# A parallel attention and linear-attention block: row maximum on other engines, sums one step later, linear outputs kept in two parts

## The chip, the cores and the metric

The kernel runs on one core of one Trainium2 chip. The metric is device time in microseconds (us): the median of several executions. A profiled execution is timed too, and the trace that is read here comes from it. The engines are named as in the profile: PE is TensorE's matmuls, PEld its weight loads, DVE is VectorE, ACT is ScalarE, POOL is GpSimd, and SP is the engine whose queue issues most transfers.

## The reference

One decoder block on 1024 tokens of width 1024, in float32. All projections come from one product with the input weights.

```python
h = rmsnorm(x, g_in)
c_q, c_kv, k_r, z_mla, q_g, k_g, v_g, a_lr, z_gla, gate_mla, gate_gla = split(h @ w_in)
# softmax attention on latent vectors, 8 heads, 64 + 32 rotary columns, causal
q = rope(rmsnorm(c_q) @ w_uq);  k, v = rmsnorm(c_kv) @ w_ukv (k with rope(k_r))
o_mla = softmax(mask(q k^T / sqrt(96))) v
y_mla = (o_mla * silu(z_mla)) @ w_proj_mla
# gated linear attention, 4 heads of 128 by 256, in chunks
log_a = log_sigmoid(a_lr @ w_gla_gate + b) / 16
o_gla = rmsnorm(linear_attention(q_g, k_g, v_g, log_a))
y_gla = (o_gla * silu(z_gla)) @ w_proj_gla
x = x + (sigmoid(gate_mla) * y_mla + sigmoid(gate_gla) * y_gla) @ w_out
return rmsnorm(x, g_final)
```

## The kernel before

The 1024 tokens are worked in two halves `h` of 512 (`TH`), one after the other. To keep float32 accuracy every operand of a large product is split into a rounded part (`hi`) and the remainder (`lo`), and `mm3` (L201) multiplies hi by hi, hi by lo and lo by hi. `split` (L210, L211) makes the parts: a cast on ScalarE and a subtract on VectorE, or on GpSimd if it is asked for.

All projections are units of one list (`Stream`): a unit loads its weights on SP's queue (L170) into one of two raw buffers, splits them (the cast at L187, the subtract at L188), and runs groups of mostly six matmuls. `st.step` gives the next group, and the other stages call it between their own steps, so that TensorE has projection matmuls to do while the attention's small steps run on other engines. `st.upto` runs all units up to a named one. The order of the instructions of each engine is laid down at build time: the framework is asked for a schedule by a simulated timeline (`schedule_with_timeline_sim=True`), with program order as the priority. On the chip every engine then runs its list in that order.

Each half has four stages.

- Start: the latent projections, the rotary tables and the decay (`decay`), which multiplies by the split gate weights `wgs` (L693) and scans with the reset row `rst` (L703). In the first half `consts` and `consts2` load the constants first, each through a staging tile of its own (`graw`, `onraw`, `sraw`).
- Linear attention, four heads (`core`). At its end each of eight feature blocks is scaled and gated into `uo` (L832) and stored in DRAM as `ugd` on SP's queue (L834).
- Softmax attention, eight heads. `row_max` makes a first, rough score product (L886) per block of 128 queries, adds the causal mask on the diagonal (L891) and takes the row maximum (L893). In the second half there are two parts of the row, whose maxima are joined (L897). The negative maximum is split into two rounded columns `mt` (L901, L902), turned by four small matmuls (L907) and copied by ScalarE into two extra rows of the query operand (L910), against which the key operand holds ones. So the score product (L930) has the maximum subtracted. `scores` then takes the exponential (L939), splits it (L942, L943) and adds it up on GpSimd (L945). The product with the values (L951, L952) is put on the list `late`, to be issued a step later; after a head's last product `finish` reads the result (L961, L962), splits the summed weights `ah` (L210, L211), and puts the product of those sums with ones (L968, L969) on the list, two steps later. `tick` counts the steps; a step is one tile of 128 keys, four to a head in the first half and eight in the second. It takes entries from the front of the list only:

```python
while late and late[0][0] <= tick_no[0]:
    late.pop(0)[1]()
```

- From the sixth head on `linear_inputs` brings the linear outputs back: one of two buffers `zr`, shared with the gate units, is loaded from `ugd` (L991) and split (L993, the subtract on GpSimd) into the latent tiles that are no longer used. After that come the output projections (L546 to L548) and the final norm.

SP's queue carries the weight loads, the stores to `ugd` and the loads from it; each waits there for its buffer. ScalarE's queue issues the gate stores, GpSimd's the key and value spills.

Of the kernel before, what the change touches and what calls it, by code (L numbers as in the profile page):

```python
# [7 lines left out]
F32 = mybir.dt.float32  # L8
F32R = mybir.dt.float32r
# [7 lines left out]
P = 128  # L17
# [110 lines left out]
def hybrid_mla_gla_block_kernel(ctx: ExitStack, tc: tile.TileContext, x, xt, pos, vec, gfin, wf, wv, wgate,  # L128
# [87 lines left out]

    def vcol(base, i=0):
        return vecs[:, base + i:base + i + 1]
# [3 lines left out]
    wgs = mk(cst, [P, 512], F32R, "wgs")  # L222
    rst = mk(cst, [P, TH], F32, "rst")
    msk = mk(cst, [P, 3, P], F32, "msk")
    onh = mk(cst, [P, 256], F32R, "onh")
# [15 lines left out]
    ugd = dram.tile([8, P, TH], F32, tag="ugd", name="ugd")  # L241
# [60 lines left out]
    def units_of(h):  # L302
# [16 lines left out]
        def latent_unit(tag, i, u0):  # L319
            @unit(f"{tag}{i}", wunit(u0 + i), "gpsimd")  # L320
            def _(w):
                yield from proj(c, w)
                if i == 0:
                    c.craw[tag] = (mk(c.pp, [P, 3, TH], F32, "craw" + tag), mk(c.pp, [P, 3, TH], F32, "csq"))
# [268 lines left out]
    def consts(bp):  # L593
# [4 lines left out]
        nc.vector.tensor_tensor(out=wgs[64:96, :], in0=graw[64:96], in1=R(wgs[64:96, :]), op=ALU.subtract)  # L598
        nc.vector.tensor_scalar(out=ggh, in0=vecs[:, V_GGLA:V_GGLA + 2], scalar1=0.5, scalar2=None, op0=ALU.mult)

    def consts2(bp):
        nc.sync.dma_start(out=rst, in_=rst_d)
        nc.sync.dma_start(out=msk, in_=msk_d)
        nc.vector.tensor_copy(out=idr, in_=idn)
        oraw = mk(bp, [P, 256], F32, "onraw")
        nc.sync.dma_start(out=oraw, in_=onh_d)
        nc.vector.tensor_copy(out=onh, in_=oraw)
        sraw = mk(bp, [48, 4, P], F32, "sraw")
# [3 lines left out]
    for h in range(2):  # L612
# [6 lines left out]
        gps = pool("glaps", 1, PSUM, stack=gs)  # L619
        um = mk(up, [P, 4, TH], F32, "um")  # L620
# [14 lines left out]
        with ExitStack() as ss:  # L635
            if h == 0:
                with ExitStack() as bs:
# [16 lines left out]
                    consts(bp)  # L654
                    for _ in pro:
                        pass
                    consts2(bp)
            c.pp = pp = pool("start", 1, stack=ss)
# [90 lines left out]
        with ExitStack() as gs2:  # L749
# [3 lines left out]
            def core(g):  # L753
# [71 lines left out]
                for vt in range(2):  # L825
# [8 lines left out]
                    nc.sync.dma_start(out=ugd[f], in_=uo)  # L834
# [9 lines left out]
        with ExitStack() as as_:  # L844
# [28 lines left out]
            def row_max(hd):  # L873
# [8 lines left out]
                for t in range(4):  # L882
                    parts = [TH] * h + [(t + 1) * P]
                    for b, n in enumerate(parts):
# [5 lines left out]
                        if b == len(parts) - 1:  # L890
                            nc.vector.tensor_tensor(out=ps[:, n - P:n], in0=ps[:, n - P:n], in1=msk[:, 1, :],  # L891
                                                    op=ALU.add)
                        nc.vector.reduce_max(mx[:, t, b:b + 1], ps[:, 0:n], axis=mybir.AxisListType.X)  # L893
                    yield
                if h == 1:
                    m1 = mk(ap2, [P, 4, 1], F32, "m1")
                    nc.vector.tensor_tensor(out=m1, in0=mx[:, :, 0:1], in1=mx[:, :, 1:2], op=ALU.max)  # L897
                else:
                    m1 = mx[:, :, 0:1]
# [265 lines left out]
```

## Time and profile before

| what | us |
|---|---|
| median of 3 executions | 1083.74 (1082.48 to 1083.81) |
| the profiled execution | 1085.81 |
| its span, first to last instruction | 1084.0 |
| TensorE's matmuls busy | 1048.3 |
| VectorE busy | 714.0 |
| ScalarE busy | 542.1 |
| GpSimd busy | 374.9 |

The span is that of the profiled execution, 1.8 us below its own time, and all rows below are read from it. Matmuls overlap in the engine's pipeline, so a row's mean duration of a matmul is longer than the time from one to the next. An idle time in brackets is that of the engine before the instruction, with the instruction or transfer that ended it.

### The profile page before, as it was taken

How to read it: one execution, taken by the hardware profiler on the slowest of the kernel's cores; microseconds unless marked ns; L12 is line 12 of the kernel's file. 1: busy time of each engine (PE TensorE's matmuls, PEld its weight loads, DVE VectorE, ACT ScalarE, POOL GpSimd, SP SyncE). 2: the span in 40 equal slices, each digit the busy share in tenths (PEclk: the TensorE clock that was granted, in tenths of full speed). 3: DMA queues.
4: the chain of work that ended last, by engine and by line, in shares of the span. 5: the costliest groups of instructions: out<-in, count | busy, mean ns of one | idle time of the engine just before them, and what ended most of it. 6: DMA issues, size and time to landing. Idle time of an engine off the chain costs nothing.

```text
span 1084.0 us, 14078 instructions
## 1 busy us (share of the span) xinstructions
PE 1048.3 (97%) x5231; PEld 872.4 (80%) x5231; DVE 714.0 (66%) x1114; ACT 542.1 (50%) x910; POOL 374.9 (35%) x274
## 2 busy tenths in 40 slices
PE   8999999999999989999999999999999998999997
PEld 5798998987778867888889989988777776788875
DVE  5796555557586776466887655455767877667673
ACT  5744334455556653444574444344664656553232
POOL 2361121114445542230524211104454656533420
PEclk8899999999999999999999999999999999899999
DMA  8213213235433446644412233235422223424532
GB/s 297 98 59 97 97 60 117 97 100 195 139 98 111 144 139 250 226 138 144 165 60 78 78 102 101 80 112 158 122 96 70 81 83 121 125 90 161 175 111 98
DMA packets 46118, 132.05 MB, mean 122 GB/s; under 512 B 5232, under 2 KB 7664, under 8 KB 45920
## 3 DMA queue, kind: packets, MB, share of 16 engines
q1 hardware_dynamic: 37760, 113.96, 32.1%
q0 software_dynamic: 3680, 8.78, 3.0%
q10 hardware_dynamic: 4608, 8.39, 2.1%
q8 instruction: 41, 0.67, 0.3%
q14 instruction: 29, 0.24, 0.1%
HBM read 110.01 MB, written 21.10 MB: 121 GB/s over the span
## 4 chain that ended last, share of the span: by engine, by line
PE 77%; DVE 12%; ACT 4%; issue 2%; DMA 2%; POOL 1%; SPq 0%; POOLq 0%; DVEq 0%; ACTq 0%
PE pj L201 58%; DVE pl L943 2%; PE y L548 2%; PE y L546 2%; PE y L547 2%; PE ops L201 2%; DVE mx L893 1%; PE sc L930 1%; PE sc L932 1%; PE sc L933 1%; PE ov L951 1%; PE ov L952 1%; PE sc L886 1%; PE at L201 1%; DVE wlo L188 1%
## 5 line engine op out<-in xcount | busy, mean ns | idle before, releaser
L201 PE MATMUL pj<-xl,whi 128*128 128x512 f32 x800 | 301.0, 399 | 1.4 <-DVE xl L282 1.4
L201 PE MATMUL pj<-xh,whi 128*128 128x512 f32 x672 | 270.5, 403 | 2.4 <-ACT whi L187 1.6
L187 ACT CAST whi<-wraw 128x1024 fp32r<-128x1024 f32 (+1 forms) x151 | 155.3, 1029 | 122.0 <-PE pj L201 91.3
L201 PEld LDWEIGHTS pj<-xl,whi 128*128 128x128 f32 x800 | 153.5, 192 | 31.9 <-DVE xl L282 2.9
L201 PE MATMUL pj<-xh,wlo 128*128 128x512 f32 x672 | 176.6, 397 | 0.0
L188 POOL TENSOR_TENSOR wlo<-wraw,whi 128x1024 fp32r<-128x1024 f32 (+2 forms) x52 | 118.2, 2274 | 140.8 <-ACT whi L187 67.4
L201 PEld LDWEIGHTS pj<-xh,whi 128*128 128x128 f32 x672 | 129.7, 193 | 28.0 <-ACT whi L187 1.9
L201 PEld LDWEIGHTS pj<-xh,wlo 128*128 128x128 f32 x672 | 127.2, 191 | 26.3
L188 DVE TENSOR_TENSOR wlo<-wraw,whi 128x1024 fp32r<-128x1024 f32 x100 | 127.4, 1275 | 21.5 <-ACT whi L187 21.3
L945 POOL TENSOR_TENSOR acc<-acc,p 128x512 f32<-128x512 f32 (+3 forms) x80 | 84.9, 1061 | 86.0 <-ACT p L939 70.5
L943 DVE TENSOR_TENSOR pl<-p,ph 128x512 fp32r<-128x512 f32 (+3 forms) x80 | 70.3, 886 | 23.4 <-ACT ph L942 23.2
L939 ACT ACTIVATE p<-sc 128x512 f32<-128x512 f32 (+3 forms) x80 | 37.3, 468 | 68.8 <-DVE sc L935 50.8
L201 PE MATMUL pj<-wlo,xh 128*128 128x256 f32 x256 | 64.4, 285 | 0.0
L201 PE MATMUL pj<-whi,xh 128*128 128x256 f32 x256 | 64.2, 284 | 0.0
L893 DVE TENSOR_REDUCE mx<-sc 128x1 f32<-128x512 f32 (+2 forms) x96 | 51.8, 551 | 11.6 <-PE sc L886 10.4
L548 PE MATMUL y<-whi,zl 128*128 128x512 f32 x128 | 50.5, 396 | 0.5 <-DVE zl L211 0.5
L547 PE MATMUL y<-wlo,zh 128*128 128x512 f32 x128 | 50.4, 395 | 0.0
L546 PE MATMUL y<-whi,zh 128*128 128x512 f32 x128 | 49.5, 396 | 0.0
L201 PEld LDWEIGHTS pj<-wlo,xh 128*128 128x128 f32 x256 | 49.0, 191 | 0.3
L201 PEld LDWEIGHTS pj<-whi,xh 128*128 128x128 f32 x256 | 48.9, 191 | 0.3
L211 POOL TENSOR_TENSOR ql<-qi,qh 128x512 fp32r<-128x512 f32 x8 | 12.4, 1554 | 93.5 <-ACT qh L210 93.5
L349 DVE TENSOR_TENSOR zr<-pj,rbc 128x512 f32<-128x512 f32 x32 | 22.0, 688 | 33.8 <-PE pj L201 33.5
(298 smaller groups left out, 2101.6 us busy)
## 6 DMA issues: line engine op xcount, KB each, us to landing
wraw<-in_dram SPq DMA_DIRECT2D x141, 512.0 KB, 3.5
gtd<-zr ACTq DMA_DIRECT2D x32, 256.0 KB, 2.2
zr<-gtd SPq DMA_DIRECT2D x32, 256.0 KB, 2.9
xr<-in_dram SPq DMA_DIRECT2D x8, 512.0 KB, 9.4
ugd<-uo SPq DMA_DIRECT2D x16, 256.0 KB, 2.2
zr<-ugd SPq DMA_DIRECT2D x16, 256.0 KB, 3.1
xo<-in_dram SPq DMA_DIRECT2D x8, 512.0 KB, 5.8
xs<-in_dram SPq DMA_DIRECT2D x7, 512.0 KB, 8.6
```

The lines of the kernel that those rows point to most:

```text
L187: nc.scalar.copy(out=hi[:, 0:n], in_=raw[:, 0:n])
L188: getattr(nc, lo_engine).tensor_tensor(out=lo[:, 0:n], in0=raw[:, 0:n], in1=R(hi[:, 0:n]), op=ALU.subtract)
L201: nc.tensor.matmul(out=ps, lhsT=a, rhs=b, start=(i == 0), stop=(i == 3 * n - 1))
L211: (lo_engine or nc.vector).tensor_tensor(out=lo, in0=src, in1=R(hi), op=ALU.subtract)
L349: nc.vector.tensor_tensor(out=zr, in0=c.ps, in1=c.rbc, op=ALU.mult)
L546: nc.tensor.matmul(out=c.ops[t], lhsT=a[0], rhs=b[0], start=(k == 0), stop=False)
L547: nc.tensor.matmul(out=c.ops[t], lhsT=a[0], rhs=b[1], start=False, stop=False)
L548: nc.tensor.matmul(out=c.ops[t], lhsT=a[1], rhs=b[0], start=False, stop=(k == 7))
L893: nc.vector.reduce_max(mx[:, t, b:b + 1], ps[:, 0:n], axis=mybir.AxisListType.X)
L939: nc.scalar.activation(p[:, 0:n], ps[:, 0:n], AF.Exp, scale=SCALE)
L943: nc.vector.tensor_tensor(out=pl[:, 0:n], in0=p[:, 0:n], in1=R(ph[:, 0:n]), op=ALU.subtract)
L945: nc.gpsimd.tensor_tensor(out=s.acc[:, q0:TH], in0=s.acc[:, q0:TH], in1=p[:, 0:n], op=ALU.add)
```

## The change

There are four parts and some moves of memory.

- `row_max`: the mask is a row `mrow` of zeros with the diagonal mask in its last 128 columns. One VectorE instruction adds its tail to the scores and takes the maximum; in the second half it starts from the maximum of the row's first part, so that the joining step goes. The two columns `mt` become the same value, minus half the maximum, by one ScalarE instruction of eight columns; the two extra rows add up to the whole.
- `finish`: the sums are due three steps later in the first half and four in the second, in place of two.
- `core`: the linear output is split there, with a cast on ScalarE and a subtract on VectorE, and `ugd` holds both parts (512 KB a block in place of 256 KB). `linear_inputs` loads the two parts straight into their places.
- Memory: `wgs` and `rst` live in the pool of the linear stage. `wgs` is stored once in DRAM and loaded again in the second half, `rst` is loaded in both. The constants share the staging tile `graw`, and the key latents' raw tile has two blocks in place of three.

```diff
+    def move(out, in_, queue=None):
+        (queue or nc.sync).dma_start(out=out.bitcast(F32), in_=in_.bitcast(F32))
-    wgs = mk(cst, [P, 512], F32R, "wgs")
-    rst = mk(cst, [P, TH], F32, "rst")
+    mrow = mk(cst, [P, TH], F32, "mrow")
-    ugd = dram.tile([8, P, TH], F32, tag="ugd", name="ugd")
+    wgd = dram.tile([96, 512], F32R, tag="wgd", name="wgd")
+    ugd = dram.tile([8, P, 2, TH], F32R, tag="ugd", name="ugd")
...
-                    c.craw[tag] = (mk(c.pp, [P, 3, TH], F32, "craw" + tag), mk(c.pp, [P, 3, TH], F32, "csq"))
+                    c.craw[tag] = (mk(c.pp, [P, 2 if tag == "ckv" else 3, TH], F32, "craw" + tag), mk(c.pp, [P, 3, TH], F32, "csq"))
...
+        move(wgd, wgs[0:96])
...
-        nc.sync.dma_start(out=rst, in_=rst_d)
         nc.sync.dma_start(out=msk, in_=msk_d)
+        nc.vector.memset(mrow, 0.0)
+        nc.vector.tensor_copy(out=mrow[:, TH - P:TH], in_=msk[:, 1, :])
         nc.vector.tensor_copy(out=idr, in_=idn)
-        oraw = mk(bp, [P, 256], F32, "onraw")
+        oraw = mk(bp, [P, 512], F32, "graw")[:, 0:256]
...
-        sraw = mk(bp, [48, 4, P], F32, "sraw")
+        sraw = mk(bp, [P, 512], F32, "graw")[0:48].rearrange("p (a b) -> p a b", a=4)
...
+        wgs = mk(gp, [P, 512], F32R, "wgs")
+        rst = mk(gp, [P, TH], F32, "rst")
...
+            if h == 1:
+                move(wgs[0:96], wgd)
+            nc.sync.dma_start(out=rst, in_=rst_d)
...
-                    nc.sync.dma_start(out=ugd[f], in_=uo)
+                    u2 = mk(gb, [P, 2, TH], F32R, "u2")
+                    split(u2[:, 0, :], u2[:, 1, :], uo)
+                    move(ugd[f], u2)
...
-                            nc.vector.tensor_tensor(out=ps[:, n - P:n], in0=ps[:, n - P:n], in1=msk[:, 1, :],
-                                                    op=ALU.add)
-                        nc.vector.reduce_max(mx[:, t, b:b + 1], ps[:, 0:n], axis=mybir.AxisListType.X)
+                            nc.vector.tensor_tensor_reduce(out=ps[:, 0:n], in0=ps[:, 0:n], in1=mrow[:, TH - n:TH], scale=1.0,
+                                                           scalar=NEG if b == 0 else mx[:, t, 0:1], op0=ALU.add,
+                                                           op1=ALU.max, accum_out=mx[:, t, b:b + 1])
+                        else:
+                            nc.vector.reduce_max(mx[:, t, b:b + 1], ps[:, 0:n], axis=mybir.AxisListType.X)
                     yield
-                if h == 1:
-                    m1 = mk(ap2, [P, 4, 1], F32, "m1")
-                    nc.vector.tensor_tensor(out=m1, in0=mx[:, :, 0:1], in1=mx[:, :, 1:2], op=ALU.max)
-                else:
-                    m1 = mx[:, :, 0:1]
                 mt = mk(ap2, [P, 4, 2], F32R, "mt")
-                nc.vector.tensor_scalar(out=mt[:, :, 0:1], in0=m1, scalar1=-1.0, scalar2=None, op0=ALU.mult)
-                nc.vector.scalar_tensor_tensor(out=mt[:, :, 1:2], in0=m1, scalar=-1.0, in1=R(mt[:, :, 0:1]),
-                                               op0=ALU.mult, op1=ALU.subtract)
+                nc.scalar.activation(mt, mx[:, :, h:h + 1].broadcast_to([P, 4, 2]), AF.Copy, scale=-0.5)
...
-                late.append((tick_no[0] + 2, sums))
+                late.append((tick_no[0] + 3 + h, sums))
...
-                    ur = mk(up, [P, TH], F32, "zr", bufs=2)
-                    nc.sync.dma_start(out=ur, in_=ugd[f])
                     hi, lo = slots[2 * f], slots[2 * f + 1]
-                    split(hi, lo, ur, nc.gpsimd)
+                    move(hi, ugd[f][:, 0, :])
+                    move(lo, ugd[f][:, 1, :])
```

## Rows read from the trace of the kernel before

**Rows 1.** The page, busy us, share of span, instructions: TensorE.

```profile
PE 1048.3 (97%) x5231; PEld 872.4 (80%) x5231; DVE 714.0 (66%) x1114; ACT 542.1 (50%) x910; POOL 374.9 (35%) x274
```

**Rows 2.** Stretches: length, busy us of each engine, PEclk, DMA share, GB/s.

```profile
120.00:160.00 40.00, 40.00 (x251) 35.93 (x250) 22.47 (x37) 17.45 (x34) 6.73 (x5) 1.00 0.28 92
...
240.00:434.00 194.00, 186.66 (x865) 150.32 (x864) 134.56 (x235) 108.80 (x179) 90.02 (x70) 0.99 0.46 152
750.00:990.00 240.00, 226.75 (x1014) 180.50 (x1013) 179.02 (x295) 137.20 (x233) 129.06 (x96) 0.98 0.33 99
380.00:410.00 30.00, 27.07 (x123) 21.31 (x122) 22.20 (x42) 17.38 (x33) 14.68 (x14) 0.94 0.39 118
...
905.00:935.00 30.00, 26.04 (x107) 20.33 (x106) 20.19 (x33) 19.20 (x34) 20.83 (x16) 0.89 0.44 132
```

**Rows 3.** Waits of TensorE: releaser, total us, times, longest us.

```profile
PE sc L907 <- DVE mt L902: 4.4, 4, 2.0
...
PE sc L886 <- ACT p L939: 2.0, 1, 2.0
PE rs L969 <- DVE ah L211: 1.8, 4, 0.9
...
PE rs L968 <- ACT ah L210: 1.5, 2, 1.3
PE ov L951 <- DVE um L962: 1.4, 1, 1.4
...
PE sc L930 <- ACT qt L910: 1.4, 4, 0.6
```

**Rows 4.** Timeline around 829 (start us, us): VectorE, GpSimd, TensorE.

```profile
826.65 0.95 DVE L901 TENSOR_SCALAR mt<-m 128x4 fp32r<-128x4 f32 x1
827.64 1.45 DVE L902 SCALAR_TENSOR_TENSOR mt<-m,mt 128x4 fp32r<-128x4 f32 x1
...
827.55 1.52 POOL L188 TENSOR_TENSOR wlo<-wraw,whi 128x640 fp32r<-128x640 f32 x1
...
829.24 0.40 PE L907 MATMUL sc<-idr,mt 128*2 128x128 f32 x4 [1.99 <-DVE mt L902]
```

**Rows 5.** Instructions of tile dec on ScalarE: ns min/median/max.

```profile
L368 ACT ACTIVATE dec<-dex x8: 189/206/214, 66.5 to 651.1; 128x5 f32<-128x5 f32 x8
```

**Rows 6.** Groups by line: count, busy us, mean ns, idle before.

```profile
L187 ACT CAST whi<-wraw 128x1024 fp32r<-128x1024 f32 (+1 forms) x151 | 155.3, 1029 | 122.0 <-PE pj L201 91.3 <-DMA wraw<-in_dram 15.7 <-issue 7.5
...
L893 DVE TENSOR_REDUCE mx<-sc 128x1 f32<-128x512 f32 (+2 forms) x96 | 51.8, 551 | 11.6 <-PE sc L886 10.4
...
L891 DVE TENSOR_TENSOR sc<-sc,msk 128x128 f32<-128x128 f32 x64 | 18.0, 290 | 6.4 <-PE sc L886 6.1
...
L902 DVE SCALAR_TENSOR_TENSOR mt<-m,mt 128x4 fp32r<-128x4 f32 x8 | 8.2, 1026 | 0.3
...
L801 ACT ACTIVATION_READ_ACCUMULATOR junk<-oraw 128x1 f32 x32 | 6.0, 188 | 0.0
...
L901 DVE TENSOR_SCALAR mt<-m 128x4 fp32r<-128x4 f32 x8 | 4.5, 561 | 0.3
```

**Rows 7.** Chain that ended last, 425 to 480: start us, us, what.

```profile
434.16 30.56 PE pj L201 x132
```

**Rows 8.** Timeline around 394: ScalarE, GpSimd, VectorE, TensorE.

```profile
391.23 0.62 ACT L210 CAST qr<-zr 128x512 fp32r<-128x512 f32 x1 [0.89 <-DMA zr<-ugd]
...
391.93 1.29 POOL L211 TENSOR_TENSOR qr<-zr,qr 128x512 fp32r<-128x512 f32 x1 [0.72 <-ACT qr L210]
...
392.41 1.36 DVE L943 TENSOR_TENSOR pl<-acc,ph 128x512 fp32r<-128x512 f32 x1 [1.65 <-ACT ph L942]
...
396.29 0.54 PE L886 MATMUL sc<-kb,qt 96*128 96x512 f32 x1 [1.97 <-ACT p L939]
```

**Rows 9.** Instructions of line L211, VectorE subtract: ns min/median/max.

```profile
L211 DVE TENSOR_TENSOR zl<-zr,zh x16: 692/905/1782, 458.4 to 1045.9; 128x512 fp32r<-128x512 f32 x16
```

**Rows 10.** Waits of SP's queue: releaser, total us, times, longest us.

```profile
SPq L834 <- DVE uo L832: 75.8, 15, 11.4
```

More of the change, by code (lines that the diff above doesn't have):

```diff
@@ L590, in hybrid_mla_gla_block_kernel, with consts @@
         st.fences |= {f"{h}{u}" for u in ("misc", "uqr", "hi0", "hi1", "hi2", "hi3", "yg0", "ym0", "wo00")}
-    def consts(bp):
+    def consts(bp, wgs):
         graw = mk(bp, [P, 512], F32, "graw")
@@ L653, in hybrid_mla_gla_block_kernel @@
                         next(pro)
-                    consts(bp)
+                    consts(bp, wgs)
                     for _ in pro:
```

## The prediction

> **What bounds the kernel now.** I read the page's busy times first. TensorE's matmuls fill nearly the whole span [rows 1], and the change adds or removes none of them: what it can win is only TensorE's idle time and its time at the lower clock. So I then asked for stretches. In the linear-attention stage TensorE never stops while VectorE and ScalarE are about half idle, as in the stretch from 120 [rows 2]; work put there is covered. In the two softmax-attention stages TensorE misses 194.00 - 186.66 = 7.3 us of the first and 240.00 - 226.75 = 13.25 us of the second, 20.6 us in all [rows 2]. VectorE is busy for 134.56 + 179.02 = 314 of those 434 us (72%), the fullest of the other engines.
>
> The last column but two of that view is the granted clock. It is below 1.00 in three places inside attention, each after a cluster of idle gaps: 0.94 over 30 us around 395 (a stretch around 830 reads the same), and 0.89 over 30 us around 920 [rows 2]. That is the lower level, 1.2 GHz, for part of each stretch. Lost there: 0.06 x 30 + 0.06 x 30 + 0.11 x 30 = 6.9 us. The most that any edit here can give back is thus 20.6 + 6.9 = 27.5 us; the start, the tail and the rest of the schedule are not touched by it.
>
> The list of waits says which releaser ends TensorE's gaps [rows 3]; all six lines lie in attention. They are the terms of the sum below.
>
> **The maximum's two roundings become one ScalarE step.** Removed: per head a multiply and a subtract on four columns on VectorE, for the second half also the maximum of two partial maxima. Added: one ScalarE copy with scale, of eight columns. The gap of 1.99 us before the transposes at 829.24 shows what this is worth [rows 4]: the two VectorE instructions begin at 826.65 and end at 829.09, 2.4 us for four columns, because each lies beside a GpSimd instruction; the subtract ends where GpSimd's 1.52 us one ends. On ScalarE a product of five columns takes 206 ns [rows 5], so the step itself is some 2.2 us shorter. It stands in ScalarE's queue, though: an instruction that waits there for the last maximum holds up the exponentials behind it, and they in turn hold up the score banks. Of the 4.4 us that L907 waits I take 3.4 as recovered (the longest gap shrinks to about 0.6, the three others to about 0.15 each), and half, 0.7, of the 1.4 us of L930 behind the next ScalarE step of the same chain [rows 3]. For the sixteen new waits on ScalarE I charge 1.0 us. Its bounds are 0, if other casts stand ahead as they do now, and 4.4, if the gap only changes its releaser.
>
> Here the Trainium skill has a rule, "SBUF — State Buffer", section "Who interferes with whom": a VectorE instruction with two SBUF inputs shares a port with GpSimd and waits for it, while ScalarE waits for no one. The trace agrees where it can: 1.45 us for four columns beside a GpSimd subtract [rows 4]. By the rule alone the whole 4.4 us would go; by the rows, 3.4 us.
>
> **Mask and maximum fused.** Removed: 64 mask additions, 18.0 us of VectorE time; 64 of the 96 maxima (mean 551 ns) become one instruction with an elementwise output and a maximum [rows 6]. The trace has no such instruction. Lower bound: it costs what the maximum of that width costs. Upper bound: a second pass over the row, another 551 ns. If it has to hand over its maximum separately, the nearest row is ScalarE's read of its accumulator, 188 ns [rows 6]. I take 0.1 us more than the maximum, so 18.0 - 6.4 = 11.6 us of VectorE time saved; the bounds are +18.0 and -17.3 us. With the small instructions of the step above (8.2 + 4.5 us of the second half [rows 6]) VectorE loses some 24 us of its 314. None of this is TensorE time by itself. I count it as the reason why the gaps above close, and add nothing.
>
> A rule of the Trainium skill speaks against this edit: "VectorE: DVE Perf Modes", section "Two Vector instructions with no wait between them", says that an instruction that also writes out its accumulator counts as two. No run here shows its price on VectorE. By it the fusion would save no instruction; with ScalarE's 188 ns the saving would be 18.0 - 12.0 = 6 us of VectorE time, and the time forecast would stay.
>
> **Key sums multiplied later.** The two matmuls that add up a head's weights (L968, L969) are put one step later in the first half and two in the second. Their inputs come over ScalarE and VectorE, and TensorE waits 1.5 + 1.8 = 3.3 us for them [rows 3]. One step there is several of the groups of six matmuls, each of these at 30.56/132 = 0.23 us a matmul [rows 7] some 1.4 us long, more than the waits. Recovered: 3.0 us. But the delayed work is a first-in first-out list, and its head is tested first. A sum that is not yet due holds back the value products behind it: one pair in the first half, two in the second, at each of seven head changes. If TensorE has nothing else to do, that is at most 7 x (1 + 2) x 2 x 0.23 = 9.7 us; if other ready work fills in, nothing. The three buffers of the attention weights' two parts are just used up then, so the next weight tile waits for the held product. I charge 1.5 us, near the lower end, since projection matmuls stand between these products everywhere.
>
> **Linear outputs stored in two parts.** Removed from attention: 16 ScalarE casts and 16 GpSimd subtracts, with the load buffer that they share with the gates. Added there: 16 more loads on SP's queue, straight into the old latent buffers. The stall at 396 shows the price of the old way [rows 8]: ScalarE stood 0.89 us waiting for the load at 391.23 with a softmax cast behind it; then the GpSimd subtract at 391.93 ran beside a VectorE subtract that took 1.36 us; TensorE stood still for 1.97 us until 396.29. I take this 2.0 us as recovered, and half, 0.7, of the 1.4 us of L951 behind L962 [rows 3], which ends a stall in the like stage of the second half. A load now waits for TensorE's last reading of its slot instead; weight loads stand behind it on SP's queue. Those readings come before the linear inputs in the program, so I charge nothing.
>
> Added in the linear-attention stage: 16 casts and 16 VectorE subtracts. A like subtract takes 0.69 to 1.78 us [rows 9]. The work that hides it is TensorE's 40.00 of 40.00 us [rows 2]; without that cover it would be 16 x (0.62 + 0.9) = 24 us. The store, twice as large, leaves some 1.5 us later, and SP already stands 75.8 us before these stores with weight loads behind them [rows 10]. But weights arrive early: the weight cast's idle time is 91.3 us for TensorE to free a buffer and 15.7 us for loads [rows 6]. I charge 0.
>
> **The rest.** The gate weights make a trip through DRAM and the reset row is loaded twice: two more loads and a store on SP, at the start of each half. The constants share one staging buffer and so load one after the other. They are needed later than the weights, so I charge 0.5 us; bounds 0 and some 3 us.
>
> **Sum.** Recovered: 3.4 + 0.7 + 3.0 + 2.7 = 9.8 us of idle time. Half of the clock loss goes with the gaps that brought it on: 3.4 us. Together 13.2 us. TensorE, released from one wait, meets the next one sooner, as the other engines are still two thirds busy: I keep 0.85 of it (a choice, no row), 11.2 us. Charges: 1.0 + 1.5 + 0.5 = 3.0 us. Left: 8.2 us. The profiled execution took 1085.81 us (span 1084.0); its median unprofiled fellow 1083.74. I take the gain off the latter: 1075.5 us, and 1075.8 for the new span.
>
> **The rivals.**
> - *The gaps only change their releaser.* The planner orders every engine anew, ScalarE takes VectorE's place before the transposes, and what is left of the gain pays the 3.0 us of charges: about 1083.5 us. For it: TensorE is 97% busy already. Against it: the longest wait ends on an instruction that no longer exists, and two others on sums that get more time.
> - *More comes back.* All 4.4 + 1.4 + 3.3 + 3.4 us of the waits and 6.9 us of clock, less 3 us: 16 us, 1067 us. For it: clock losses follow the gaps. Against it: the releasers that stay, as the additions of the causal mask.
> - *Slower: value products held behind the sums.* The place is the list of delayed work, the price up to 9.7 us of idle time, which just cancels the 11.2 - 1.5 us that the other terms leave. Gaps of that kind bring the clock down as around 920, 3.3 us each time; two such falls make it 1090 us. It decides where a head change costs over 9.7/14 = 0.7 us. Against it: ready projection matmuls.
> - *The fused step makes two passes.* VectorE then has 17 us more from it and 13 less from the small ones; the chain of the maxima is longer by 0.55 us for each head's last tile, which takes back the first term, 0.85 x 4.1 = 3.5 us: 1079 us, inside the likeliest case.
>
> **How the numbers follow.** Likeliest, with its bounds (charges 0 to 6, clock 0 to 6.9): 0.58, from 1083.7 - 0.85 x 16.7 = 1069.5 to 1083.7 - 0.85 x 9.8 + 6 = 1081.5 us. The gaps change their releaser: 0.15. More comes back: 0.14. Slower: 0.13, of which value products 0.09 and weight loads late behind the stores 0.04. A measurement of this kernel can tell some 0.2%, 2.2 us, from no change. So faster 0.72, same 0.15, slower 0.13. The range takes in the likeliest case, most of the equal one and half of the better one: 1066 to 1085 us.
>
> **What would show it.** Right: no wait of L907's transposes over 0.7 us, no wait of the sums, no ScalarE wait for a stored linear output, a granted clock of 1.00 around 395 and 830, TensorE idle below 13 us in the two stages, nothing lost in the linear stage. Wrong: new gaps before L951 at head changes, exponentials waiting behind the ScalarE step, the fused step far over 0.7 us, weight casts waiting for loads after the stores, or a stretch of the lower clock at a new place.

## The result and the profile after

The kernel after takes 1068.26 us (median of 4 runs, 1066.45 to 1069.86) against 1083.11 us of the kernel before in the same series (4 runs, 1081.53 to 1083.81): a ratio of 0.987 [0.9852, 0.9888], 14 to 15 us less. The forecast was 1075.5 us with a range of 1066 to 1085. Direction, place and range hold; the gain is nearly double the 8.2 us of the sum, and the time lies below the likeliest case, which ended at 1069.5 us. The profiled execution took 1068.33 us with a span of 1066.2, so the two spans differ by 17.8 us, some 3 us more than the medians do. Read the stages below with that in mind.

The page after, engines and one line of the DMA issues:

```profile
PE 1033.9 (97%) x5231; PEld 863.6 (81%) x5231; DVE 695.4 (65%) x1092; ACT 544.4 (51%) x926; POOL 352.7 (33%) x258
...
ugd<-u SPq DMA_DIRECT2D x16, 512.0 KB, 3.9
```

TensorE has the same 5231 matmuls as in [rows 1], yet is busy 14.4 us less. To compare stages fairly the stretches must end at the same instructions: the softmax attention is taken from VectorE's half of the split of the rotary key (`krs`, L211) to the reciprocal of the summed weights. First before, then after, in the columns of [rows 2]; the first row and the last two of after answer to rows shown there.

```profile
238.20:418.60 180.40, 173.06 (x811) 140.51 (x810) 125.93 (x229) 105.03 (x175) 86.24 (x67) 0.99 0.42 133
737.00:993.40 256.40, 243.16 (x1090) 194.05 (x1089) 186.02 (x307) 145.04 (x244) 135.60 (x102) 0.98 0.35 105
```

```profile
120.00:160.00 40.00, 40.00 (x251) 35.90 (x250) 24.14 (x39) 18.59 (x36) 6.72 (x5) 1.00 0.30 105
...
238.60:413.80 175.20, 170.76 (x816) 140.33 (x815) 111.21 (x216) 104.08 (x178) 75.36 (x59) 1.00 0.46 154
730.20:973.60 243.40, 236.45 (x1087) 190.25 (x1086) 178.58 (x285) 143.31 (x246) 125.46 (x93) 1.00 0.39 120
...
380.00:410.00 30.00, 28.57 (x143) 23.45 (x142) 19.58 (x41) 16.84 (x33) 6.17 (x8) 1.00 0.40 126
...
890.00:925.00 35.00, 34.59 (x164) 27.52 (x163) 26.78 (x42) 22.92 (x41) 15.80 (x13) 1.00 0.61 203
```

What to see: the first attention went from 180.40 to 175.20 us, the second from 256.40 to 243.40, 18.2 us together; all other stages together changed by 0.4 us (more on these below). Within the 18.2, TensorE's idle time fell from 20.6 to 11.4 us (9.2 less) and its busy time from 416.2 to 407.2 us (9.0 less). The granted clock reads 1.00 in both stages, where it was 0.99 and 0.98, and the two stretches that read 0.94 and 0.89 in [rows 2] have no counterpart. VectorE's busy time in them fell by 22.2 us (24 forecast).

The 0.4 us of the other stages hides two opposite changes. Outside attention TensorE's idle time rose from 15.1 to 20.9 us and its busy time fell from 632.1 to 626.7 us, with a higher granted clock there too. The stages ahead of each attention show most of it, first before, then after:

```profile
0.00:238.20 238.20, 231.53 (x1293) 200.02 (x1294) 147.83 (x231) 117.25 (x201) 54.21 (x37) 0.96 0.34 115
418.60:737.00 318.40, 317.24 (x1685) 271.06 (x1685) 202.21 (x287) 146.19 (x249) 74.83 (x52) 0.99 0.38 128
```

```profile
0.00:238.60 238.60, 229.51 (x1294) 197.99 (x1295) 149.69 (x240) 120.37 (x207) 54.02 (x37) 0.98 0.35 122
413.80:730.20 316.40, 312.50 (x1680) 268.03 (x1679) 204.62 (x294) 147.91 (x254) 73.78 (x53) 1.00 0.40 135
```

TensorE's waits after:

```profile
PE tr L261 <- DVE f3q L735: 5.7, 2, 3.2
PE sc L938 <- ACT p L947: 2.5, 4, 0.9
...
PE sc L899 <- ACT kb L491: 1.9, 2, 1.6
PE sc L899 <- DVE mx L904: 1.6, 2, 1.3
...
PE rs L977 <- DVE ah L211: 0.2, 1, 0.2
...
PE sc L938 <- ACT qt L918: 0.2, 1, 0.2
```

Of the six lines in [rows 3], 12.5 us together, 0.4 us is left. The transposes (now L915) wait for nothing. Part came back under other names: the scores behind the exponentials (L938 behind L947) take 2.5 us, the rough scores behind the keys' copies and the maxima (L899) 1.9 and 1.6; 1.28 of the latter is before the very matmul that waits 1.97 us in [rows 8]. The first line is new and not in attention: at the start of each half the transposes that spread the query latent's norm factor `f3q` wait up to 3.2 us. VectorE's timeline there, first before (L720, L724), then after:

```profile
65.57 0.15 DVE L720 TENSOR_TENSOR f2q<-at,f1q 128x4 f32<-128x4 f32 x1
...
67.36 1.18 DVE L724 TENSOR_TENSOR f3q<-f3q,rcol 128x4 f32<-128x4 f32 x1
```

```profile
58.79 6.67 DVE L714 TENSOR_TENSOR_SCAN S<-rst,mn 128x512 f32<-128x512 f32 x4
...
66.09 0.14 DVE L731 TENSOR_TENSOR f2q<-at,f1q 128x4 f32<-128x4 f32 x1
66.16 1.21 DVE L188 TENSOR_TENSOR wlo<-wraw,whi 128x1024 fp32r<-128x1024 f32 x1
...
70.53 0.15 DVE L735 TENSOR_TENSOR f3q<-f3q,rcol 128x4 f32<-128x4 f32 x1
```

The decay's four scans run in one block, and between the two small steps of the factor stand a weight subtract and the decay's next steps; they begin 4.4 us apart, where it was 1.8 us before.

How the fused step runs, by lines (columns as in [rows 6]):

```profile
L187 ACT CAST whi<-wraw 128x1024 fp32r<-128x1024 f32 (+1 forms) x151 | 155.2, 1029 | 107.8 <-PE pj L201 73.8 <-DMA wraw<-in_dram 16.8 <-PE y L552 7.0
...
L908 DVE TENSOR_REDUCE mx<-sc 128x1 f32<-128x512 f32 x32 | 21.8, 685 | 9.3 <-PE sc L899 9.1
...
L904 DVE CUSTOM_DVE_ANT_0 sc<-sc,mrow,mx 128x128 f32<-128x128 f32 (+3 forms) x32 | 17.6, 551 | 1.7 <-PE sc L899 0.3
L904 DVE CUSTOM_DVE_ANT_0 sc<-sc,mrow 128x128 f32<-128x128 f32 (+3 forms) x32 | 15.6, 497 | 3.9 <-PE sc L899 3.9
...
L904 DVE DVE_READ_ACCUMULATOR2_ANT mx<- 128x1 f32 x64 | 8.8, 137 | 0.1
```

One instruction of the program is two on the engine: the pass over the row and a read of its accumulator, 137 ns. Together 17.6 + 15.6 + 8.8 = 42.0 us. Before, the same work was 18.0 us of additions and 51.8 - 21.8 = 30.0 us of maxima [rows 6], 48.0 us. VectorE saves 6.0 us, not the 11.6 forecast: the pass is some 0.05 us longer than the maximum on the mean and the read comes on top, 0.19 us for each of the 64 where 0.1 was taken.

The chain to the transposes in the second half, timeline from 817 (VectorE, ScalarE, TensorE):

```profile
817.39 0.68 DVE L908 TENSOR_REDUCE mx<-sc 128x1 f32<-128x512 f32 x1
...
818.19 0.75 DVE L904 CUSTOM_DVE_ANT_0 sc<-sc,mrow,mx 128x512 f32<-128x512 f32 x1
818.86 0.14 DVE L904 DVE_READ_ACCUMULATOR2_ANT mx<- 128x1 f32 x1
...
819.79 0.21 ACT L911 ACTIVATE mt<-mx 128x8 fp32r<-128x8 f32 x1
...
820.22 0.41 PE L915 MATMUL sc<-idr,mt 128*2 128x128 f32 x4
```

The pass takes 0.75 us where the plain maximum of the same width takes 0.68: there is no second pass. The step on ScalarE waits 0.79 us for its turn behind other casts, takes 0.21, and TensorE has other matmuls meanwhile: no bracket stands behind its line, where [rows 4] has 1.99 us.

### The profile page after: what moved, and what is told of

Same layout as the page of the kernel before. It is cut to its first block, busy times and chain, and to the rows that moved or that the text cites. A ratio compares the mean times of both kernels' runs of the same rounds, so it can differ in the third digit from the quotient of the medians.

```text
span 1066.2 us, 14119 instructions
## 1 busy us (share of the span) xinstructions
PE 1033.9 (97%) x5231; PEld 863.6 (81%) x5231; DVE 695.4 (65%) x1092; ACT 544.4 (51%) x926; POOL 352.7 (33%) x258
## 4 chain that ended last, share of the span: by engine, by line
PE 75%; DVE 13%; ACT 4%; DMA 4%; issue 3%; POOL 1%; SPq 0%; POOLq 0%; DVEq 0%; ACTq 0%
PE pj L201 55%; PE ops L201 2%; DMA zr<-gtd 2%; PE y L552 2%; PE y L550 2%; DVE pl L951 2%; PE y L551 2%; DVE wlo L188 2%; PE sc L938 1%; PE sc L940 1%; PE sc L941 1%; PE ov L959 1%; PE ov L960 1%; PE sc L899 1%; DVE zl L211 1%
## 5 line engine op out<-in xcount | busy, mean ns | idle before, releaser
L201 PE MATMUL pj<-xl,whi 128*128 128x512 f32 x800 | 297.1, 394 | 0.7 <-DVE xl L286 0.6
L201 PE MATMUL pj<-xh,whi 128*128 128x512 f32 x672 | 266.7, 397 | 2.2 <-ACT whi L187 2.2
L201 PEld LDWEIGHTS pj<-xl,whi 128*128 128x128 f32 x800 | 151.3, 189 | 30.6 <-DVE xl L286 2.1
L201 PE MATMUL pj<-xh,wlo 128*128 128x512 f32 x672 | 173.3, 392 | 0.0
L201 PEld LDWEIGHTS pj<-xh,whi 128*128 128x128 f32 x672 | 127.4, 190 | 26.1 <-ACT whi L187 2.5
L201 PEld LDWEIGHTS pj<-xh,wlo 128*128 128x128 f32 x672 | 125.0, 188 | 25.6
L951 DVE TENSOR_TENSOR pl<-p,ph 128x512 fp32r<-128x512 f32 (+3 forms) x80 | 78.6, 991 | 28.3 <-ACT ph L950 27.5
L947 ACT ACTIVATE p<-sc 128x512 f32<-128x512 f32 (+3 forms) x80 | 37.1, 467 | 64.3 <-DVE sc L943 48.7
L211 POOL TENSOR_TENSOR ql<-qi,qh 128x512 fp32r<-128x512 f32 x8 | 13.2, 1650 | 91.9 <-ACT qh L210 91.9
L533 POOL TENSOR_TENSOR zr<-zr,xh 128x512 f32<-128x512 f32 x16 | 27.8, 1754 | 41.1 <-DVE zr L532 41.1
```

Of the source, the lines that this page charges most:

```text
L201: nc.tensor.matmul(out=ps, lhsT=a, rhs=b, start=(i == 0), stop=(i == 3 * n - 1))
L211: (lo_engine or nc.vector).tensor_tensor(out=lo, in0=src, in1=R(hi), op=ALU.subtract)
L533: nc.gpsimd.tensor_tensor(out=t2, in0=t2, in1=c.m2[:, j, :], op=ALU.add)
L947: nc.scalar.activation(p[:, 0:n], ps[:, 0:n], AF.Exp, scale=SCALE)
L951: nc.vector.tensor_tensor(out=pl[:, 0:n], in0=p[:, 0:n], in1=R(ph[:, 0:n]), op=ALU.subtract)
```

## The experiments

Each kernel was run in five rounds beside the kernel before, on the same chip (medians of before there: 1081.59 to 1081.75 us). A ratio is to before, with its 95% interval. "Attention" is the time of both stages between the two landmarks above, from the one profiled execution of each kernel. All else together takes from 643 to 650 us in these executions (`l_only` left out), so attention is the sharper number for a cause in it, and the ratio the one for the whole. It is a single execution each time: those of before (1085.81 us) and `mem_only` (1088.41) lie 2 us or more above their medians, and `s_only`, whose time is that of before, reads 1.6 us less. Differences of 1 to 2 us in this column show little.

The expectations missed more often than they hit. `m_only` and `t_mem` came out faster than either range, `m_load` between its two; `no_m`, `no_t`, `no_s`, `no_l`, `m_dve` and `l_only` fell in the range of the rival, the last for another reason than it gave. Only `m_t` and `mem_only` came in the range first named; `s_only` just missed it.

| kernel | ratio | median us | attention us |
|---|---|---|---|
| before | 1 | 1081.6 (1083.11 beside after) | 436.8 |
| moves of memory alone (`mem_only`) | 1.0021 [1.0007, 1.0036] | 1083.73 | 436.7 |
| ScalarE step alone (`m_only`) | 0.993 [0.9913, 0.9947] | 1074.37 | 427.3 |
| the same, old VectorE work kept (`m_load`) | 0.9952 [0.9936, 0.9969] | 1076.89 | 430.0 |
| sums later alone (`s_only`) | 0.999 [0.9979, 1.0002] | 1081.03 | 435.2 |
| linear outputs alone (`l_only`) | 1.0024 [1.0013, 1.0036] | 1084.20 | not comparable |
| fused step on the moves (`t_mem`) | 0.9945 [0.9922, 0.9967] | 1075.50 | 426.9 |
| ScalarE step and fused step on the moves (`m_t`) | 0.9881 [0.9859, 0.9904] | 1068.94 | 421.2 |
| after | 0.987 [0.9852, 0.9888] | 1068.26 | 418.6 |
| after without the ScalarE step (`no_m`) | 0.9886 [0.9869, 0.9903] | 1069.11 | 423.4 |
| after without the fused step (`no_t`) | 0.9902 [0.9886, 0.9918] | 1070.84 | 422.9 |
| after without later sums (`no_s`) | 0.9854 [0.9838, 0.9871] | 1065.76 | 418.7 |
| after without two-part outputs (`no_l`) | 0.9893 [0.9876, 0.9909] | 1069.46 | 421.1 |
| after, the step on VectorE (`m_dve`) | 0.9879 [0.9858, 0.99] | 1068.98 | 419.1 |

**Each part alone on the kernel before.** The ScalarE step:

```diff
-                nc.vector.tensor_scalar(out=mt[:, :, 0:1], in0=m1, scalar1=-1.0, scalar2=None, op0=ALU.mult)
-                nc.vector.scalar_tensor_tensor(out=mt[:, :, 1:2], in0=m1, scalar=-1.0, in1=R(mt[:, :, 0:1]),
-                                               op0=ALU.mult, op1=ALU.subtract)
+                nc.scalar.activation(mt, m1.broadcast_to([P, 4, 2]), AF.Copy, scale=-0.5)
```

> The kernel before with one part alone: the two columns of the maximum come from one ScalarE step (minus half the maximum, twice), the maxima and all else as before. Theory of waits: the 4.4 us of TensorE's waits for the two VectorE roundings and most of the 1.4 us behind them go, with the lower clock around 830 (1.8 us): 1076 to 1079 us. Rival, new order: the waits only find another releaser, and the time stays within 2 us of 1083.

The windows of its two attentions:

```profile
236.90:414.70 177.80, 172.78 (x811) 141.49 (x810) 120.25 (x213) 106.45 (x183) 86.93 (x67) 0.98 0.42 135
731.90:981.40 249.50, 240.47 (x1090) 191.87 (x1089) 179.34 (x291) 145.03 (x251) 135.50 (x102) 0.99 0.36 108
```

7.3 us by the medians; in attention 9.5, of which TensorE's idle time gives 20.6 - 14.1 = 6.5. Of the two waits it was meant for, that of the transposes fell from 4.4 to 0.3 us, but the 1.4 us behind it, for `qt`, stayed. Other waits went in its place: those of the sums, 3.3 us in [rows 3], fell to 0.9, and that behind `um`, 1.4 us, is gone. The lower clock is still there, at other places than before (0.98 in the first attention, 0.99 in the second).

The later sums:

```diff
-                late.append((tick_no[0] + 2, sums))
+                late.append((tick_no[0] + 3 + h, sums))
```

> The kernel before with the key sums due one step later in the first half and two in the second, nothing else. Theory of waits: the 3.3 us of waits for the sums go and perhaps half of the 3.3 us of clock around 920: 1078 to 1081 us. Rival, held products: the value products behind the sums in the list cost as much or more, 1083 to 1090 us, with new waits before L951 at head changes.

Its waits of TensorE:

```profile
PE sc L907 <- DVE mt L902: 4.4, 4, 1.9
...
PE rs L969 <- DVE ah L211: 1.9, 4, 0.9
...
PE rs L968 <- ACT ah L210: 1.5, 2, 1.3
```

The two waits of the sums stand as in [rows 3], 1.9 and 1.5 us, at the same four heads: there TensorE still begins the second product 0.1 us after VectorE's split has ended. The later place in the program did not make TensorE reach them later relative to their inputs, and the time is the same.

The two-part linear outputs, with none of the memory moves:

```diff
-                    nc.sync.dma_start(out=ugd[f], in_=uo)
+                    u2 = mk(gb, [P, 2, TH], F32R, "u2")
+                    split(u2[:, 0, :], u2[:, 1, :], uo)
+                    move(ugd[f], u2)
...
-                    ur = mk(up, [P, TH], F32, "zr", bufs=2)
-                    nc.sync.dma_start(out=ur, in_=ugd[f])
                     hi, lo = slots[2 * f], slots[2 * f + 1]
-                    split(hi, lo, ur, nc.gpsimd)
+                    move(hi, ugd[f][:, 0, :])
+                    move(lo, ugd[f][:, 1, :])
```

> The kernel before with the linear outputs stored and loaded in two parts, nothing else (no constants moved). Theory of waits: the stalls around 395 and 920 go, some 5 us of idle time with 1.8 to 5 us of clock: 1073 to 1078 us, and TensorE stays at full in the linear stage. Rival: the 16 casts and subtracts and the later store cost in the linear stage what they save in attention, 1082 to 1086 us.

The tile `krs` in this kernel (ns, first and last start), then its waits:

```profile
L211 DVE TENSOR_TENSOR krs<-krr,krs x2: 682/686/689, 238.2 to 755.1; 32x512 fp32r<-32x512 f32 x2
```

```profile
PE pj L201 <- DVE vm L459: 4.3, 3, 2.0
...
PE sc L892 <- DVE mx L899: 3.5, 3, 2.2
PE sc L892 <- ACT kb L491: 2.3, 2, 1.6
```

The first attention is 2.2 us shorter (178.2 for 180.4); of the stall of 1.97 us in [rows 8], 1.10 us is left at that place, behind exponentials. The linear stage costs nothing here either: from 600 us on TensorE is busy for 136.00 of 136.00 us. In the second half the order of the instructions came out anew: the split of the rotary key starts at 755.1 in place of 737.0. TensorE's waits for values (`vm`), maxima (`mx`) and keys (`kb`), 4.3, 3.5 and 2.3 us, were 2.2, 1.3 and 0.8 in the kernel before, and 2.6 us is lost on the whole. That the new order is what costs it is the likely reading; no run held the order fixed. It is the rival "the gaps only change their releaser" for this edit by itself. The late split also shifts the landmark, so no attention time is given.

**The moves and the fused step.** `mem_only` is after with its four parts undone, so that the gate weights' trip, the shared staging and the reloads stay. `t_mem` adds the fused step to it, with the two VectorE roundings, the sums two steps later and the linear outputs whole.

> The kernel after with its four parts undone: only the memory moves stay (gate weights stored in DRAM and loaded again, reset row loaded twice, constants through one staging tile, the mask row made but not used). Theory: 0 to 1 us slower than before, 1083 to 1084.5 us, the start of a half a little later. Rival, new order: another plan for all engines moves the time by 3 us or more either way.

> The fused mask and maximum alone, on the memory moves that it needs (mem_only), with the two VectorE roundings, whole linear outputs and the sums as before. mem_only took 1083.7 us. Theory of parts that help each other: the fused instruction shortens VectorE's way to the maximum by one instruction per block, so a part of what the ScalarE step alone gave (7 us) comes here too: 1077 to 1081 us, with fewer waits for the maxima. Rival: 6 us less VectorE work off the path gives nothing, 1082 to 1085 us.

Waits of `mem_only`, then the two attentions of `mem_only` and of `t_mem`:

```profile
PE tr L261 <- DVE f3q L735: 5.9, 2, 3.3
PE sc L918 <- DVE mt L913: 4.1, 4, 2.0
...
PE rs L980 <- DVE ah L211: 1.8, 4, 0.9
```

```profile
238.20:418.60 180.40, 173.92 (x811) 141.60 (x811) 124.69 (x230) 105.08 (x175) 86.88 (x67) 0.98 0.42 132
738.80:995.10 256.30, 243.19 (x1090) 193.85 (x1089) 185.78 (x307) 144.94 (x243) 134.68 (x100) 0.98 0.35 104
...
238.50:417.20 178.70, 173.61 (x816) 141.68 (x815) 118.25 (x229) 105.11 (x176) 87.00 (x67) 0.99 0.42 136
733.40:981.60 248.20, 238.37 (x1089) 192.16 (x1088) 181.70 (x299) 145.45 (x243) 138.03 (x100) 0.99 0.35 107
```

The moves cost some 2 us, and bring the new wait of L261 at the starts; attention is untouched (436.7). On that ground the fused step by itself gives 0.9945/1.0021 = 0.992, 8 us, and 9.8 us in attention. The waits behind `mt` halve from 4.1 to 2.0 us and those of the sums all but go (0.4 us), although their instructions are the same. Of the 9.8 us, TensorE's idle time gives 4.7 (19.6 to 14.9) and its busy time 5.1 (417.1 to 412.0), with the granted clock up from 0.98 to 0.99. So an edit that saves six us of VectorE time, before the transposes and before the splits of the sums, gave that much. How much of it is the time saved and how much the order, which came out anew, is open: in the two traces some 220 of the 5231 matmuls stand at another place in TensorE's list, where it is some 45 between before and `m_only`.

`m_t` has the ScalarE step and the fused step, and neither of the other parts:

> The kernel after without the two-part linear outputs and with the sums due as before: the ScalarE step and the fused maximum alone, on the memory moves. Theory: these two are nearly the whole gain, 1067 to 1071 us. Rival: the linear outputs' part, which alone was 2.6 us slower, is needed as well, 1071 to 1076 us.

```profile
237.10:413.00 175.90, 170.69 (x811) 139.65 (x811) 113.23 (x214) 105.90 (x183) 86.10 (x67) 1.00 0.42 136
730.40:975.70 245.30, 237.88 (x1090) 191.88 (x1089) 176.97 (x283) 145.84 (x251) 135.62 (x100) 0.99 0.36 109
```

0.9881 is nearly the whole change (0.987), and nearly the product of the two alone, 0.993 x 0.9945 = 0.9875: by the ratios they simply add up. In attention they give 15.5 us of the 18.2, where apart they gave 9.5 and 9.8. By these single executions the overlap is in the idle time, 6.5 and 4.7 us apart and 7.0 together (19.6 to 12.6), as either edit shortens the waits of the transposes and of the sums; the busy time, 3.0 and 5.1 us apart, gives 8.5 together.

**After without one part.** Each of the four edits was undone by itself in the kernel after: the two roundings on VectorE from the fused maximum (`no_m`); addition, maximum and joining step with the ScalarE step kept (`no_t`); the sums two steps later (`no_s`); the linear outputs whole, split in attention (`no_l`).

> The kernel after, but the two columns of the maximum are made on VectorE again (multiply, then subtract), from the fused maximum. Theory of waits: TensorE waits again some 3 to 4 us before the transposes, and the lower clock may come back once: 1071 to 1075 us. Rival, new order: within 2 us of 1068.

> The kernel after, but mask addition and maximum are two instructions again, with the joining step of the second half. The fused instruction took 0.5 us with a read of 0.14 us behind it, 42 us in all, against 30 us + 18 us for the two: VectorE has 6 us less to do in the kernel after. Theory: next to nothing, 1068 to 1070 us. Rival: the joined maximum is on the way to the transposes, so 2 to 4 us slower, 1070 to 1072 us.

> The kernel after, but the key sums are due two steps later as before. Theory of waits: 2 to 4 us slower, 1070 to 1072 us, with waits of the sums for VectorE. Rival, held products: the value products are no longer held, and the time falls below 1067 us.

> The kernel after, but the linear outputs are stored whole and split in attention again, on ScalarE and GpSimd. Theory of waits: the stalls of ScalarE for the loads come back, 5 to 8 us slower, 1073 to 1076 us, most of it after the fifth head of either half. Rival, new order: within 2 us of 1068.

In attention, undoing the ScalarE step costs 4.8 us, the fused step 4.3, the linear outputs 2.5 and the later sums 0.1. By the ratios the first three cost 0.16, 0.32 and 0.23%, 1.7 to 3.5 us, with intervals that overlap that of after. In attention each costs about half of what it gave alone (4.8 for 9.5, 4.3 for 9.8), as the others cure a part of the same waits: without the ScalarE step the transposes wait 2.0 us, not the 4.4 of before. `no_s` has the lowest ratio of all, 0.16% or 1.7 us below after, but the intervals overlap too: [0.9838, 0.9871] and [0.9852, 0.9888]. Its attention does not differ, and its waits of the sums are these:

```profile
PE rs L977 <- DVE ah L211: 0.2, 1, 0.2
```

So the sums stop waiting without being moved at all. What changed is when their inputs are ready. At the first head of the first half VectorE's split of the sums ran like this before, then in `no_s`:

```profile
296.14 2.46 DVE L211 TENSOR_TENSOR ah<-acc,ah 128x512 fp32r<-128x512 f32 x1 [1.98 <-ACT ah L210]
...
290.87 2.28 DVE L211 TENSOR_TENSOR ah<-acc,ah 128x512 fp32r<-128x512 f32 x1
```

The head's last product with the values ended at 295.61 and at 294.02 us. So the split ended 3.0 us after it before, and 0.9 us ahead of it in `no_s`. Whether leaving them where they were is really faster stays open; it is not slower, and it is the best version that was run.

**Why one step is better than two.** Either ScalarE is the point (its step doesn't meet GpSimd), or that there is one step, or that VectorE has less to do. `m_dve` is after with the step on VectorE:

```diff
-                nc.scalar.activation(mt, mx[:, :, h:h + 1].broadcast_to([P, 4, 2]), AF.Copy, scale=-0.5)
+                nc.vector.tensor_scalar(out=mt, in0=mx[:, :, h:h + 1].broadcast_to([P, 4, 2]), scalar1=-0.5, scalar2=None, op0=ALU.mult)
```

> The kernel after, but the one step that makes both columns (minus half the maximum, eight columns) runs on VectorE instead of ScalarE. Theory of the other engine: VectorE's step is held beside GpSimd's instructions and stands behind its queue, 2 to 4 us slower than after, 1070 to 1072 us. Rival: that there is one step in place of two is what counts, 1067 to 1069 us.

`m_load` is `m_only` with the two old VectorE instructions put back after the ScalarE step, into a tile `md` that nothing reads. That work is added and changes no result:

```diff
+                md = mk(ap2, [P, 4, 2], F32R, "md")
+                nc.vector.tensor_scalar(out=md[:, :, 0:1], in0=m1, scalar1=-1.0, scalar2=None, op0=ALU.mult)
+                nc.vector.scalar_tensor_tensor(out=md[:, :, 1:2], in0=m1, scalar=-1.0, in1=R(md[:, :, 0:1]),
+                                               op0=ALU.mult, op1=ALU.subtract)
```

> The kernel before with the ScalarE step as in m_only, but VectorE still does the two old roundings, into a tile that nothing reads. It has VectorE's old load with the new, short way to the transposes. Theory of the way: what counts is that the transposes no longer wait behind VectorE, so the time is that of m_only, 1073 to 1076 us. Rival, theory of the load: what counts is VectorE's time, held beside GpSimd, so the gain goes and the time is 1079 to 1083 us.

The step's instruction in after (ns min/median/max), and in `m_dve`:

```profile
L911 ACT ACTIVATE mt<-mx x16: 198/209/211, 272.4 to 944.4; 128x8 fp32r<-128x8 f32 x16
```

```profile
L911 DVE TENSOR_SCALAR mt<-mx x16: 152/171/1137, 271.4 to 945.4; 128x8 fp32r<-128x8 f32 x16
```

On VectorE the step takes up to 1.14 us, on ScalarE always some 0.2; still `m_dve` is as fast as after (0.9879 and 0.987; 419.1 and 418.6 us of attention), and its transposes wait 0.2 us. The ratios of `no_m` (0.9886), `m_dve` and after can't be told apart; the profiled executions can: two instructions on VectorE leave 2.0 us of waits before the transposes and 423.4 us of attention, one leaves 0.2 and 419.1. As far as these show it, one instruction in place of two is what counts here, not the engine.

`m_load` keeps 5 of the 7 us of `m_only` (6.8 of 9.5 in attention). Here the order did not come out anew: in the two traces each engine runs the same instructions in the same order, with the 32 old ones put in between on VectorE. So the difference, some 2.5 us, is VectorE's load alone. The 5 us that stay are the shorter way to the transposes, with whatever the order of `m_only` gave. The two intervals overlap, so the shares are rough.

## Why the prediction held, and where its sum was off

**Place and direction: right; the size is that of a rival.** 1068.26 us lies below the likeliest case (1069.5 to 1081.5 us, chance 0.58). It is the time of the rival "more comes back" (1067 us, chance 0.14), and the range holds it only because half of that rival was taken in. What that rival says did come about in attention: nearly all of the waits listed went, some to come back under other names, and all of the clock. The gain is in the two attentions, half of it idle time and half busy time of TensorE; nothing is lost in the linear stage (40.00 of 40.00 us busy from 120, and 138.00 of 138.00 from 590 in the second half, with the added casts and subtracts). Of the signs named, these came: no wait of the transposes, no wait of the sums over 0.2 us, a clock of 1.00 around 395 and in all of attention, and 11.4 us of idle time (below 13). Weight casts wait 16.8 us for loads, against 15.7 in [rows 6]: the charge of 0 for the larger stores was right.

**Row maximum by one step: right, price too low.** The wait was put at 3.4 of 4.4 us recovered and 0.7 of 1.4 behind it; 4.4 and 1.2 went. But the 1.2 us is not this edit's: with the ScalarE step alone (`m_only`) the 1.4 us stays, and without it (`no_m`) the wait is gone all the same, so that term was right by luck. Why the way is short was put in part on ScalarE's freedom from GpSimd; `m_dve` shows no time that this adds. The charge of 1.0 us for ScalarE's queue did not come: the scores wait 2.5 us for exponentials in after and 2.2 us in `m_dve`, which has no such step on ScalarE.

**Mask and maximum fused: the step that failed.** "I count it as the reason why the gaps above close, and add nothing" was wrong in the sum: alone it gives some 8 us. It does so through the waits that the sum credits to other edits and through the clock; the share of the new order is open, as said above. The VectorE time was wrong the other way, 6.0 us saved for 11.6. That all of VectorE lost 22.2 us in attention where 24 was forecast is chance. The forecast counted the small steps of the second half alone, 12.7 us, while those of both halves went, 18.9 us and 1.3 for the joining step; and the softmax subtract (L943, now L951) took 78.6 us in place of 70.3. The rule of the Trainium skill set beside it ("VectorE: DVE Perf Modes", "Two Vector instructions with no wait between them", that an instruction with an accumulator output counts as two) agrees with the trace in the separate read, of 137 ns. The 6 us that the estimate by it gave is met by luck: it took 188 ns for the read and nothing for a longer pass. The smaller saving won the larger time; that it did so because it lies ahead of the waits is argued, not shown. The rival "two passes" is excluded by 0.75 us against 0.68.

**Sums later: right amount, wrong cause.** 3.0 us were credited to the later place; 3.1 of 3.3 us went. `s_only` shows that the later place alone removes none, and `no_s` that without it they go as well, as their inputs come earlier. The held value products, charged 1.5 us and the ground of the slower rival, cost nothing to be seen: 418.6 us of attention with, 418.7 without.

**Linear outputs: right amount in the whole change, by luck.** 2.7 us were forecast and undoing it takes 2.5 us more in attention, but the waits that it was read from do not bear it out. The stall of 1.97 us in [rows 8] was taken as recovered; the same matmul, the last rough score of the first half, still waits 1.28 us in after, now for the maximum:

```profile
392.18 0.50 PE L899 MATMUL sc<-kb,qt 96*128 96x512 f32 x1 [1.28 <-DVE mx L904]
```

The 0.7 us read from the wait behind `um` is not this edit's doing either, as that wait is gone in `no_l` too. And the edit has a cost: the first rough score of the first half waits 1.6 us for the keys in after and in `l_only`, 0.5 in before and in `no_l`. Where the 2.5 us come from stays open. Alone it is slower, most likely because the order of the second half came out anew. This was seen as a general rival, not as one of this edit.

**Clock and knock-on: the size.** Half of 6.9 us was taken to come back; the granted clock of 1.00 says that all did. It took more than one edit: with the ScalarE step alone the two attentions read 0.98 and 0.99, with the fused step alone 0.99 and 0.99. TensorE's busy time fell by 9.0 us in attention. The 2 us beyond the 6.9 may be the ends of matmuls that no longer stand alone before a gap; this is argued, not shown. Of idle time, six waits gave 12.1 us and 2.9 came back elsewhere, so 0.76 was kept where 0.85 was chosen. Against the sum for attention, 11.2 - 2.5 = 8.7 us, the profiled pair gained 18.2: idle time 9.2 where 8.3 - 2.5 = 5.8 was counted, busy time 9.0 where 2.9 was.

**The moves: too cheap.** 0.5 us was charged within bounds of 0 to 3; they cost some 2 us, with waits of about 3 us before the transposes at the start of each half. The prediction also held that "the start, the tail and the rest of the schedule are not touched by it". TensorE stands idle outside attention for 20.8 us in `mem_only` and 20.9 in after, against 15.1 before; that after is not slower there by as much is due to 5.4 us less busy time, which no term forecast. What is late there is no load but a small step in VectorE's list, as shown above. The prediction looked at the loads alone; which of the moves puts VectorE's list in that order was not tried.

## What to carry to other kernels

When an engine feeds the bound engine through many short chains, time saved on it just ahead of the waits can be worth more than its own length: an edit that saved 6 us of VectorE time gave some 8 us here, about half of it in busy time at a higher clock, though the order of instructions changed with it. Terms read from a list of waits should not be tied to one edit each; test them by taking each edit out and putting each in, since cures can overlap (6.5 and 4.7 us of idle time apart, 7.0 together) and a wait can be cured by another edit than the one it was credited to. An edit that is good in the whole may be bad alone where the order of instructions is planned anew with every build.

## What the runs showed of the hardware

VectorE's fused addition and maximum appears as one pass (0.75 us for 128 x 512 from the scores' bank, 0.68 for the plain maximum) and a separate read of 137 ns. A VectorE instruction of only eight columns with one tensor input took from 152 to 1137 ns, while ScalarE's of the same shape took 198 to 211.
